# Expert 1's low parts on VectorE, counting products later, and each place finished within the next place's gate and up products

## The chip, the cores and the metric

The kernel runs on one core of a Trainium2 chip. The metric is the device time in microseconds (us) of one execution. The engines are named as in the profile: PE (TensorE), DVE (VectorE), ACT (ScalarE), POOL (GpSimd) and SP (SyncE). POOL, SP and ACT also issue DMAs.

## The reference

One decoder layer over 2,048 tokens and 16 meta tokens, all in float32, width 1,024. After a mixer come a residual sum, a normalization, routing, 16 small experts, and a last normalization:

```
g_sel = argmax(g_logits)                          # one of 4 groups
top_p, top_i = top_k(softmax(e_logits of that group), 2)   # two of its 4 experts
weights = p_g * top_p / sum(top_p)
for e in range(16):
    h = silu(xt @ w_gate[e]) * (xt @ w_up[e])     # 1024 -> 256
    y = y + combine[:, e:e+1] * (h @ w_down[e])   # 256 -> 1024
out = rmsnorm(h + y, final_norm_w)[:, 16:]
```

So each token goes through two experts, and its output can be normalized only when both have been added.

## The kernel before, in words

PE multiplies at a reduced precision, so every float32 operand is split into a high part (rounded, mostly on ACT, L107 and L111) and a low part (the remainder, L108 and L112, on DVE), and each product is three matmuls: high by high, low by high, high by low.

The first two thirds of the time are the mixer and the routing, over 16 token tiles of 128. `route_rest` writes for each tile the tokens' records to a table in DRAM (POOL, L690), sorted by expert and slot: for the tile's chosen experts `A` it needs the number of tokens that each expert has had before (products with `before_b` and `ones_b`), and for the last tile the total counts too (`counts`), from which `rank_experts` ranks the experts by size.

The experts then run one after the other in "places" 0 to 15. Places 0 and 1 are experts 0 and 1, the others are ordered by count. Places below 10 have three row tiles (128, 128 and 64 tokens), the others two. For a place

- `load_places` (SP) loads its part of the table to SBUF, `fix_words` (DVE, L1115 to L1121) turns the words into row numbers: word 1 for a token's first expert, word 2 for its second,
- `gather` (POOL, L924) fetches the tokens' rows, xg<-hn_dram,
- `transposes` (PE L946) turns them, with the split on ACT (L107) and DVE (L108),
- `gate_up` computes the hidden values in two halves f = 0, 1 (PE L975 to L977; then ACT L981, DVE L982, and the split of the hidden value: high on ACT L957, low on DVE L959 and L961),
- `down` does the down products for all row tiles, first with half 0 and then with half 1 (PE L1036 to L1041), with the result weighted and copied out by ACT (L1052) or DVE (L1054) into a row tile `xr`; when a row tile is complete POOL scatters the rows of first experts into a DRAM accumulator, oe<-xr, and gathers-and-adds that accumulator to the rows, xr<-oe,
- `square` (ACT L1072) sums the squares of the result, and `finish` (DVE: L1089, a reciprocal square root by L59 to L67, then L1078) scales it; POOL stores it, out_dram<-xr.

Rows that are not wanted have row numbers out of range, so every place issues all of these. There are six `xr` row tiles. PSUM banks are few and named: mm (two), sp, o, ds, tp, zg, m2 (shown as m). The transposes of the next place use tp and zg, which the down products use too.

The call `between(i)` inside the products of a place does the next place's transposes, one split of raw weights (`split_chunk`: ACT L111, DVE L112) and its loads. Places 0 and 1 start early: their first 13 token tiles' rows are gathered before the routing ends (`gate_rows(0, 0)`, `gate_rows(0, 2)`, then place 1's), and their second row tile (`gate_rows(0, 1)`) once all tables are there. Four of expert 1's weight chunks are split with the low part on POOL. A scheduler sets the final order of instructions on each engine; `must_follow` adds a wait.

Of the kernel before, what the change touches and what calls it, by code (L numbers as in the profile page):

```python
# [12 lines left out]
OP = mybir.AluOpType  # L13
# [4 lines left out]
NT = 16  # L18
# [3 lines left out]
NE = 16  # L22
# [48 lines left out]
def body(ctx, tc, I, O):  # L71
    nc = tc.nc
    V = nc.vector
# [14 lines left out]
    def must_follow(ins, earlier):  # L88
        for o_ in earlier:
            tc.add_manual_dep(ins.ins, o_.ins.name,  # L90
                              mybir.DependencyInfo(mybir.DependencyClass.Sync, mybir.DependencyReason.DATA),
                              reason="rows written through indices")
# [63 lines left out]
    iota16 = iota("iota16", 16, 1)  # L156
    FIXED = 2
# [462 lines left out]
    def route_rest(t):  # L620
# [9 lines left out]
        if t == EARLY + 1:  # L630
            nc.tensor.matmul(pp[:, 1], ones_b, acc[i % 2], start=True, stop=True)
            early = pp[:, 1]
            V.tensor_copy(counts, early)
            for row, at in ((late1, 128.0), (late2, float(SMALL)), (late3, float(CAP))):
                V.tensor_scalar(row[:, FIXED:], early[:, FIXED:], -1.0, at, op0=OP.mult, op1=OP.add)
            V.tensor_scalar(late2[:, :FIXED], early[:, :FIXED], -1.0, float(CAP), op0=OP.mult, op1=OP.add)
            V.tensor_scalar(late2[:, :FIXED], late2[:, :FIXED], 128.0, None, op0=OP.min)
            V.tensor_copy(late3[:, :FIXED], late2[:, :FIXED])
            V.scalar_tensor_tensor(late0[:, FIXED:], early[:, FIXED:], 48.0, iota16[:, FIXED:], op0=OP.mult, op1=OP.add)
        elif t == NT:  # L640
            nc.tensor.matmul(pp[:, 1], ones_b, acc[i % 2], start=True, stop=False)
            nc.tensor.matmul(pp[:, 1], ones_b, A, start=False, stop=True)
            V.tensor_tensor(counts, pp[:, 1], counts, op=OP.add)
        pp = pp[:, 0]
        picked[0] = nc.tensor.matmul(pp, before_b, A, start=True, stop=(t == EARLY + 1))
        if t != EARLY + 1:
            nc.tensor.matmul(pp, ones_b, acc[i % 2], start=False, stop=True)
        ngm, eg, sg, nm1, p2, den, w = T("ngm", 1), T("eg", 4), T("sg", 1), T("nm1", 1), T("p2", 1), T("den", 1), T("w", 2)
        V.tensor_scalar(ngm, gm, -1.0, None, op0=OP.mult)
        nc.scalar.activation(eg, lg[:, 0:4], AF.Exp, bias=ngm, accum_out=sg)  # L650
# [114 lines left out]
    def split_chunk(eng=None):  # L765
        r = chunks[done[0]]
        kind, e, i = stream[done[0]]
        done[0] += 1
        if kind == "d":
            hi, lo = DW[i]  # L770
        else:
            hi, lo = WP[i] if e % 2 == 0 else (WB[i][h][:, :1024] for h in range(2))
        return split(hi, lo, r, eng)
# [130 lines left out]
    with ExitStack() as c2:  # L904
# [82 lines left out]
        def gate_rows(e, j, tag, between=None):  # L987

            n, p = rows[j], bank(tag)
            for k in range(KB):  # L990
                if between:
                    between(k)
                wh, wl = gate_slot(e, k)
                xh, xl = (x[:, cols[j]:cols[j] + n] for x in XE[e % 2][k])
                nc.tensor.matmul(p[:n], xh, wh, start=(k == 0), stop=False)
                nc.tensor.matmul(p[:n], xl, wh, start=False, stop=False)
                gate_ops[k] = nc.tensor.matmul(p[:n], xh, wl, start=False, stop=(k == KB - 1))
            return j, p
# [70 lines left out]
        def square(e, j):  # L1069
            n = rows[j]  # L1070
            sq = mk.tile([128, D], BF, name="sq")
            s_ = nc.scalar.activation(sq[:n], RT[e][j][:n], AF.Square, accum_out=SS[e % 2][:n, part[j]:part[j] + 1])  # L1072
            if e + 2 < NE:
                must_follow(s_, hidden_done)
# [60 lines left out]
            for k in range(KB):  # L1135
                transposes(0, k, (0, 2), added[0])
        early = [gate_rows(0, 0, "mm"), gate_rows(0, 2, "mm", lambda k: k < 6 or transposes(1, k - 6, (0, 2)))]
        must_follow(picked[0], [gate_ops[2]])
        for k in range(4):
            split_chunk(nc.gpsimd)  # L1140
            load_chunks(min(8 + k, 10))
        for k in range(2, KB):
            transposes(1, k, (0, 2))
        load_places(0, FIXED, slice(0, FIXED))
        fix_words(0, FIXED, iota16)
        for e in range(FIXED, NE):
            load_places(e, e + 1, expert(e))
        first_rows = [ind(XG[e][1], hn_dram, col(e, 1, 0), False) for e in range(2)]
# [16 lines left out]
                    transposes(0, i, (1,))  # L1165

        early_1 = [gate_rows(1, 0, "sp"), gate_rows(1, 2, "o", early_rest)]
        down(0, (0, 2))
        for e in range(NE):
            def between(i):  # L1170
                if e + 1 < NE and i % 2 == 0:
                    for k in range(i, i + 2):
                        transposes(e + 1, k, None if e else (1,))
                if e == 0:
                    if i in (2, 6):
                        fix_words(*((2, 9) if i == 2 else (9, 16)), place)
                    if i == 0:
                        for op in load_chunks(10 + WRB, mk):
                            must_follow(op, first_rows)
                else:  # L1180
                    if done[0] < len(stream) and (i < 2 if e == NE - 1 else i in (0, 1, 2, 3, 4, 6)):
                        gate = stream[done[0]][0] == "g"
                        for op in split_chunk():
                            if gate:
                                must_follow(op, hidden_done)
                        load_chunks(done[0] + WRB, mk)
                if e >= NE - 2 and i == 1:
                    RT[e] = [row_tile(True) for j in JS[e]]
                    for j in JS[e]:
                        add_oe(e, ind(RT[e][j][:rows[j]], oe, col(e, j, 0), False), True)  # L1190
            if e == NE - 1:
                first = gate_rows(e, 0, "mm", between)
                second = gate_rows(e, 1, "mm", lambda k: k != 3 or hidden_rows(*first))
                with tc.high_priority():
                    hidden_rows(*second)
                down(e, (0,))
                down(e, (1,))
                break
            if e > 1:
                gate_up(e, between)  # L1200
            else:
                late_rows = gate_rows(e, 1, "mm", between)
                for j, p in (early_1 if e else []) + [late_rows]:
                    hidden_rows(j, p)
            if e + 3 < NE:
                gather(e + 3)
            if e > 1:
                for j in JS[e - 1]:
                    square(e - 1, j)
            if e == NE - 2:  # L1210
                finish(e - 1)
            down(e, None if e else (1,))
            if 1 < e < NE - 2:
                finish(e - 1)
            if e == 8:
                count_left(mk)

# [132 lines left out]
```

## Time and profile before

| | |
|---|---|
| timed, median of 3 | 1127.59 us (1126.79 to 1127.94) |
| profiled execution | 1121.29 us, span 1119.5 us |
| PE busy | 1055.8 us (94%) |
| DVE busy | 779.8 us (70%) |
| ACT busy | 565.7 us (51%) |
| POOL busy | 313.8 us (28%) |

The span is that of the profiled execution, from its first to its last instruction; what lies around it makes up the rest of that execution's time. Issuing a DMA on POOL shows as a busy time of its own (L690, L924), its landing comes later and is given with the DMA issues.

### The profile page before, as it was taken

How to read it: one execution, taken by the hardware profiler on the slowest of the kernel's cores; microseconds unless marked ns; L12 is line 12 of the kernel's file. 1: busy time of each engine (PE TensorE's matmuls, PEld its weight loads, DVE VectorE, ACT ScalarE, POOL GpSimd, SP SyncE). 2: the span in 40 equal slices, each digit the busy share in tenths (PEclk: the TensorE clock that was granted, in tenths of full speed). 3: DMA queues.
4: the chain of work that ended last, by engine and by line, in shares of the span. 5: the costliest groups of instructions: out<-in, count | busy, mean ns of one | idle time of the engine just before them, and what ended most of it. 6: DMA issues, size and time to landing. Idle time of an engine off the chain costs nothing. (4 is left out here: it accounts for less than half of the span.)

```text
span 1119.5 us, 19115 instructions
## 1 busy us (share of the span) xinstructions
PE 1055.8 (94%) x6614; PEld 946.5 (85%) x6614; DVE 779.8 (70%) x2649; ACT 565.7 (51%) x1192; POOL 313.8 (28%) x276
## 2 busy tenths in 40 slices
PE   7999999999999999999999998879999999989982
PEld 5888888888888889999999998558998899988861
DVE  6476666545555776878777788747787788867873
ACT  7545444334433643333333334337767777667741
POOL 2000000000000000121111105524677777776551
PEclk9999999999999999999999999989999999989996
DMA  8412332111121352533434344488888997889852
GB/s 279 166 66 76 107 101 90 62 57 48 67 85 57 115 196 67 170 142 120 145 124 151 114 153 160 132 235 237 221 248 230 242 264 214 231 256 311 255 152 74
DMA packets 64471, 174.09 MB, mean 156 GB/s; under 512 B 21012, under 2 KB 21317, under 8 KB 64368
## 3 DMA queue, kind: packets, MB, share of 16 engines
q1 hardware_dynamic: 36272, 105.72, 27.7%
q0 software_dynamic: 25504, 58.53, 20.0%
q10 hardware_dynamic: 2592, 8.55, 2.1%
q8 instruction: 54, 0.88, 0.3%
q14 instruction: 49, 0.40, 0.1%
HBM read 143.74 MB, written 57.74 MB: 180 GB/s over the span
## 5 line engine op out<-in xcount | busy, mean ns | idle before, releaser
L441 POOL DMA_DIRECT2D y_dram<-y x16 | 8.6, 541 | 391.2 <-DVE y L439 391.2
L924 POOL DMA_INDIRECT oe<-xr,tab x40 | 69.3, 1732 | 69.0 <-ACT xr L1052 57.3
L321 PE MATMUL mm<-wb,XL 128*128 128x512 f32 (+1 forms) x240 | 83.6, 348 | 0.0
L322 PE MATMUL mm<-wb,XH 128*128 128x512 f32 (+1 forms) x240 | 83.0, 346 | 0.0
L690 POOL DMA_INDIRECT table<-rec,ix x32 | 33.3, 1042 | 176.8 <-DVE tmp L703 85.4
L320 PE MATMUL mm<-wb,XH 128*128 128x512 f32 (+1 forms) x240 | 82.2, 342 | 0.0
L924 POOL DMA_INDIRECT xr<-oe,tab x39 | 75.4, 1932 | 17.8 <-issue 9.8
L523 PE MATMUL mm<-XL,ws 128*128 128x256 f32 (+1 forms) x256 | 73.0, 285 | 0.2 <-DVE XL L112 0.2
L522 PE MATMUL mm<-XH,ws 128*128 128x256 f32 (+1 forms) x256 | 73.0, 286 | 0.0
L524 PE MATMUL mm<-XH,ws 128*128 128x256 f32 (+1 forms) x256 | 72.2, 282 | 0.0
L111 ACT ACTIVATE XH<-xt 128x1024 fp32r<-128x1024 f32 x32 | 33.8, 1058 | 56.4 <-PE mm L524 36.0
L924 POOL DMA_INDIRECT out_dram<-xr,tab x39 | 55.6, 1426 | 20.8 <-DVE sr_y L60 7.4
L975 PE MATMUL mm<-xh,ws 128*128 128x320 f32 (+1 forms) x168 | 51.3, 306 | 0.0
L976 PE MATMUL mm<-xl,ws 128*128 128x320 f32 (+1 forms) x168 | 51.2, 305 | 0.0
L977 PE MATMUL mm<-xh,ws 128*128 128x320 f32 (+1 forms) x168 | 51.0, 304 | 0.0
L320 PE MATMUL mm<-ws,XH 128*128 128x512 f32 x112 | 47.4, 423 | 2.0 <-ACT XH L111 2.0
L321 PEld LDWEIGHTS mm<-wb,XL 128*128 128x128 f32 x240 | 45.4, 189 | 4.4
L1078 DVE SCALAR_TENSOR_TENSOR xr<-xr,sr_y,fw 128x1024 f32<-128x1024 f32 (+1 forms) x39 | 48.7, 1278 | 0.5
L320 PEld LDWEIGHTS mm<-wb,XH 128*128 128x128 f32 x240 | 45.1, 188 | 4.6
L322 PEld LDWEIGHTS mm<-wb,XH 128*128 128x128 f32 x240 | 45.1, 188 | 4.5
L523 PEld LDWEIGHTS mm<-XL,ws 128*128 128x128 f32 x256 | 48.1, 188 | 0.7 <-DVE XL L112 0.4
L524 PEld LDWEIGHTS mm<-XH,ws 128*128 128x128 f32 x256 | 48.4, 189 | 0.3 <-issue 0.2
(654 smaller groups left out, 3840.8 us busy)
## 6 DMA issues: line engine op xcount, KB each, us to landing
raw<-in_wgu_e_dram SPq DMA_DIRECT2D x42, 512.0 KB, 5.2
xt<-in_xT_dram SPq DMA_DIRECT2D x32, 512.0 KB, 3.5
xn<-in_xn_dram SPq DMA_DIRECT2D x32, 512.0 KB, 3.5
wr<-in_wgu_e_dram SPq DMA_DIRECT2D x22, 512.0 KB, 5.9
raw<-in_wd_e_dram SPq DMA_DIRECT2D x20, 512.0 KB, 5.6
hn_dram<-xn ACTq DMA_DIRECT2D x16, 512.0 KB, 3.3
oe<-xn POOLq DMA_DIRECT2D x16, 512.0 KB, 3.7
wr<-in_wd_e_dram SPq DMA_DIRECT2D x12, 512.0 KB, 5.8
```

The lines of the kernel that those rows point to most:

```text
L111: return (nc.scalar.activation(hi, src, AF.Copy), (eng or V).tensor_tensor(lo, src, hi.bitcast(F32), op=OP.subtract))
L320: nc.tensor.matmul(q, xh[:, k, :], wh[:, c0:c1_], start=(k == 0), stop=False)
L321: nc.tensor.matmul(q, xl[:, k, :], wh[:, c0:c1_], start=False, stop=False)
L322: nc.tensor.matmul(q, xh[:, k, :], wl[:, c0:c1_], start=False, stop=(k == KB - 1))
L522: nc.tensor.matmul(ps[:, b], WS[k][0][:, c], XH[:, k, o:], start=(k == 0), stop=False)
L523: nc.tensor.matmul(ps[:, b], WS[k][0][:, c], XL[:, k, o:], start=False, stop=False)
L524: nc.tensor.matmul(ps[:, b], WS[k][1][:, c], XH[:, k, o:], start=False, stop=(k == KB - 1))
L924: return nc.gpsimd.indirect_dma_start(out=out_, out_offset=off if scatter else None, in_=in_, in_offset=None if scatter else off, bounds_c ...
L975: nc.tensor.matmul(p[:, c0:c1_], wh, xh, start=(k == 0), stop=False)
L976: nc.tensor.matmul(p[:, c0:c1_], wh, xl, start=False, stop=False)
L977: nc.tensor.matmul(p[:, c0:c1_], wl, xh, start=False, stop=(k == KB - 1))
L1078: V.scalar_tensor_tensor(x[:n], x[:n], r[:n], fw[:n], op0=OP.mult, op1=OP.mult)
```

## The change

In `route_rest`, the two counting products of the last tile come after the products that give the slots, and the marked product of the last tile (`picked`) follows step 6 of the steps 0 to 7 of `gate_rows(0, 2)` (`gate_ops[6]`) where it followed step 2. The four splits of expert 1's weights have their low parts on DVE, and wait for the end of the routing. `fix_words` for places 0 and 1 comes later in the code, that for places 2 to 15 within place 1's products, not place 0's. `square` and `finish` of place e-1 are called within `gate_up` of place e, before the sixth and the seventh of its eight steps, for e from 2 to 14; before, `square` was called after `gate_up` and `finish` after `down` (for place 14 before it).

```diff
@@ -637,14 +637,14 @@
             V.tensor_scalar(late2[:, :FIXED], late2[:, :FIXED], 128.0, None, op0=OP.min)
             V.tensor_copy(late3[:, :FIXED], late2[:, :FIXED])
             V.scalar_tensor_tensor(late0[:, FIXED:], early[:, FIXED:], 48.0, iota16[:, FIXED:], op0=OP.mult, op1=OP.add)
-        elif t == NT:
-            nc.tensor.matmul(pp[:, 1], ones_b, acc[i % 2], start=True, stop=False)
-            nc.tensor.matmul(pp[:, 1], ones_b, A, start=False, stop=True)
-            V.tensor_tensor(counts, pp[:, 1], counts, op=OP.add)
-        pp = pp[:, 0]
+        total, pp = pp[:, 1], pp[:, 0]
         picked[0] = nc.tensor.matmul(pp, before_b, A, start=True, stop=(t == EARLY + 1))
         if t != EARLY + 1:
             nc.tensor.matmul(pp, ones_b, acc[i % 2], start=False, stop=True)
+        if t == NT:
+            nc.tensor.matmul(total, ones_b, acc[i % 2], start=True, stop=False)
+            nc.tensor.matmul(total, ones_b, A, start=False, stop=True)
+            V.tensor_tensor(counts, total, counts, op=OP.add)
         ngm, eg, sg, nm1, p2, den, w = T("ngm", 1), T("eg", 4), T("sg", 1), T("nm1", 1), T("p2", 1), T("den", 1), T("w", 2)
         V.tensor_scalar(ngm, gm, -1.0, None, op0=OP.mult)
         nc.scalar.activation(eg, lg[:, 0:4], AF.Exp, bias=ngm, accum_out=sg)
@@ -1135,14 +1135,13 @@
             for k in range(KB):
                 transposes(0, k, (0, 2), added[0])
         early = [gate_rows(0, 0, "mm"), gate_rows(0, 2, "mm", lambda k: k < 6 or transposes(1, k - 6, (0, 2)))]
-        must_follow(picked[0], [gate_ops[2]])
+        must_follow(picked[0], [gate_ops[6]])
         for k in range(4):
-            split_chunk(nc.gpsimd)
+            must_follow(split_chunk()[1], [routed])
             load_chunks(min(8 + k, 10))
         for k in range(2, KB):
             transposes(1, k, (0, 2))
         load_places(0, FIXED, slice(0, FIXED))
-        fix_words(0, FIXED, iota16)
         for e in range(FIXED, NE):
             load_places(e, e + 1, expert(e))
         first_rows = [ind(XG[e][1], hn_dram, col(e, 1, 0), False) for e in range(2)]
@@ -1165,15 +1164,16 @@
                     transposes(0, i, (1,))
 
         early_1 = [gate_rows(1, 0, "sp"), gate_rows(1, 2, "o", early_rest)]
+        fix_words(0, FIXED, iota16)
         down(0, (0, 2))
         for e in range(NE):
             def between(i):
                 if e + 1 < NE and i % 2 == 0:
                     for k in range(i, i + 2):
                         transposes(e + 1, k, None if e else (1,))
+                if e == 1 and i in (2, 6):
+                    fix_words(*((2, 9) if i == 2 else (9, 16)), place)
                 if e == 0:
-                    if i in (2, 6):
-                        fix_words(*((2, 9) if i == 2 else (9, 16)), place)
                     if i == 0:
                         for op in load_chunks(10 + WRB, mk):
                             must_follow(op, first_rows)
@@ -1184,6 +1184,11 @@
                             if gate:
                                 must_follow(op, hidden_done)
                         load_chunks(done[0] + WRB, mk)
+                if 1 < e < NE - 1 and i == 5:
+                    for j in JS[e - 1]:
+                        square(e - 1, j)
+                if 1 < e < NE - 1 and i == 6:
+                    finish(e - 1)
                 if e >= NE - 2 and i == 1:
                     RT[e] = [row_tile(True) for j in JS[e]]
                     for j in JS[e]:
@@ -1204,14 +1209,7 @@
                     hidden_rows(j, p)
             if e + 3 < NE:
                 gather(e + 3)
-            if e > 1:
-                for j in JS[e - 1]:
-                    square(e - 1, j)
-            if e == NE - 2:
-                finish(e - 1)
             down(e, None if e else (1,))
-            if 1 < e < NE - 2:
-                finish(e - 1)
             if e == 8:
                 count_left(mk)
 
```

What the change does to the order at three places follows; DMA rows name the destination and the source.

On DVE, between the routing and place 0's second row tile: L108 on `xl` of 128 columns are the eight low parts of that tile's transposes, and L1115 of 336 columns starts `fix_words` for places 2 to 8. Before:

```order
L1004 TENSOR_TENSOR h<-mm,h 64x256
L112 TENSOR_TENSOR HB<-tp,HB 128x2x64
L1115 TENSOR_TENSOR sq<-tab,iota_114 128x336
L108 SCALAR_TENSOR_TENSOR xl_8621<-zg,vecs,xh_8620 128x128
L108 SCALAR_TENSOR_TENSOR xl_8621<-tp,vecs,xh_8620 128x128
L1116 TENSOR_TENSOR sq<-sq,place 128x336
```

With the change:

```order
L1004 TENSOR_TENSOR h<-mm,h 64x256
L108 SCALAR_TENSOR_TENSOR xl_8621<-zg,vecs,xh_8620 128x128
L112 TENSOR_TENSOR HB<-tp,HB 128x2x64
L108 SCALAR_TENSOR_TENSOR xl_8621<-zg,vecs,xh_8620 128x128
L108 SCALAR_TENSOR_TENSOR xl_8621<-tp,vecs,xh_8620 128x128
L1115 TENSOR_TENSOR sq<-tab,iota_114 128x336
L108 SCALAR_TENSOR_TENSOR xl_8621<-zg,vecs,xh_8620 128x128
L1116 TENSOR_TENSOR sq<-sq,place 128x336
```

Three of the eight low parts have moved ahead of L1115; before, all eight stood behind it.

On POOL, one place of the steady part: the scatters and gathers of a place e, and the three stores (x3) of place e-1. Before:

```order
L924 DMA oe<-xr,tab 2048x1024
L924 DMA xr<-oe,tab 128x1024
L924 DMA oe<-xr,tab 2048x1024
L924 DMA xr<-oe,tab 128x1024
L924 DMA oe<-xr,tab 2048x1024
L924 DMA xr<-oe,tab 64x1024
L924 DMA out_dram<-xr,tab 2048x1024 x3
```

With the change:

```order
L924 DMA out_dram<-xr,tab 2048x1024 x3
L924 DMA oe<-xr,tab 2048x1024
L924 DMA xr<-oe,tab 128x1024
L924 DMA oe<-xr,tab 2048x1024
L924 DMA xr<-oe,tab 128x1024
L924 DMA oe<-xr,tab 2048x1024
L924 DMA xr<-oe,tab 64x1024
```

The three stores have moved from behind the six scatters and gathers to ahead of them. So it is for places 2 to 7; from place 8 on, the stores stand behind the first scatter, or the first scatter and gather.

On ACT and DVE, the same part: the second half of a place's hidden value (ACT L981, L957; DVE L982, L959, L961), the squares (L1072) and the finish (L1089 to L1078) of the place before. ACT before, and with the change:

```order
L981 ACTIVATE h<-mm 128x320
L107 ACTIVATE xh_8620<-tp,vecs 128x320
L107 ACTIVATE xh_8620<-zg,vecs 128x320
L957 ACTIVATE HB<-h 128x320
L1072 ACTIVATE sq,SS_8877<-xr 128x1024
```

```order
L981 ACTIVATE h<-mm 128x320
L1072 ACTIVATE sq,SS_8869<-xr 128x1024
L107 ACTIVATE xh_8620<-tp,vecs 128x320
L1072 ACTIVATE sq,SS_8869<-xr 64x1024
L107 ACTIVATE xh_8620<-zg,vecs 128x320
L957 ACTIVATE HB<-h 128x320
```

DVE with the change:

```order
L1089 SCALAR_TENSOR_TENSOR ms<-SS_8869,tab 128x3
L59 TENSOR_SCALAR sr_y<-ms 128x3
L60 TENSOR_SCALAR sr_y<-sr_y 128x3
L108 SCALAR_TENSOR_TENSOR xl_8621<-zg,vecs,xh_8620 128x320
L982 TENSOR_TENSOR h<-m_10370,h 128x320
L65 TENSOR_TENSOR sr_t<-sr_y 128x3
L66 TENSOR_TENSOR sr_t<-sr_t,ms 128x3
L67 SCALAR_TENSOR_TENSOR sr_y<-sr_t,sr_y 128x3
L65 TENSOR_TENSOR sr_t<-sr_y 128x3
L959 TENSOR_TENSOR HB<-h,HB 128x256
L961 TENSOR_TENSOR HB<-h,HB 128x64
L66 TENSOR_TENSOR sr_t<-sr_t,ms 128x3
```

On ACT the third square, which needs the third gather of the place before, now stands ahead of the hidden value's high part (L957). On DVE the hidden value's L982, L959 and L961, which stood ahead of L1089 and next to each other, now stand behind it.

## Rows read from the trace of the kernel before

**Rows 1.** By stretch: busy us of PE, PEld, DVE, ACT, POOL; clock, DMA, GB/s.

```profile
900.00:980.00 80.00, 79.63 (x516) 73.45 (x516) 67.03 (x143) 58.09 (x100) 57.98 (x37) 1.00 0.83 231
```

**Rows 2.** Timeline of PE: start, us, operation, idle before, its releaser.

```profile
708.67 0.17 PE L642 MATMUL m<-A,ones_b 128*128 128x16 bf16 x1 [2.70 <-DVE A L615]
...
735.34 0.47 PE L946 MATMUL zg<-ident,xg 128*128 128x128 f32 x1 [7.04 <-DVE xl L108]
...
744.83 0.48 PE L995 MATMUL mm<-ws,xh 128*128 128x512 f32 x1
```

**Rows 3.** Timeline of POOL, end of routing.

```profile
695.47 2.43 POOL L112 TENSOR_TENSOR wb<-raw,wb 128x1024 fp32r<-128x1024 f32 x1 [6.59 <-PE ds L572]
```

**Rows 4.** Timeline of DVE, routing to the second half of expert 0.

```profile
696.61 1.32 DVE L663 TENSOR_TENSOR v<-v,late 128x16 f32<-128x16 f32 x1
...
697.93 2.29 DVE L665 TENSOR_TENSOR t<-t,step 128x16 f32<-128x16 f32 x1
...
700.23 2.35 DVE L667 TENSOR_TENSOR t<-lev,late_step 128x16 f32<-128x16 f32 x1
...
708.97 2.28 DVE L685 TENSOR_SCALAR rec<-w,rs_r 128x2 f32<-128x2 f32 x1
...
711.60 0.16 DVE L665 TENSOR_TENSOR t<-t,step 128x16 f32<-128x16 f32 x1
...
715.04 1.22 DVE L112 TENSOR_TENSOR wb<-raw,wb 128x1024 fp32r<-128x1024 f32 x1
...
734.51 0.51 DVE L1115 TENSOR_TENSOR sq<-tab,iota 128x336 f32<-128x336 f32 x1 [7.33 <-DMA tab<-table]
```

**Rows 5.** Timeline of PE, places 7, 9 and 13.

```profile
913.14 0.39 PE L1036 MATMUL sp<-wb,HB 128*128 128x512 f32 x1
...
916.84 0.40 PE L1036 MATMUL sp<-wb,HB 128*128 128x512 f32 x1
...
961.82 0.39 PE L1036 MATMUL sp<-wb,HB 128*128 128x512 f32 x1
...
1048.64 0.39 PE L1036 MATMUL sp<-wb,HB 128*128 128x512 f32 x1
```

**Rows 6.** Timeline of POOL, places 1, 6 and 8.

```profile
786.45 1.73 POOL L924 DMA_INDIRECT xr<-oe,tab  x1 [0.30 <-issue]
...
895.81 1.59 POOL L924 DMA_INDIRECT oe<-xr,tab  x1 [2.91 <-ACT xr L1052]
...
906.75 1.74 POOL L924 DMA_INDIRECT xr<-oe,tab  x1 [0.30 <-issue]
...
908.79 1.04 POOL L924 DMA_INDIRECT out_dram<-xr,tab  x1 [0.30 <-issue]
...
911.99 1.76 POOL L924 DMA_INDIRECT out_dram<-xr,tab  x1 [0.30 <-DVE xl L108]
...
945.32 1.61 POOL L924 DMA_INDIRECT oe<-xr,tab  x1 [4.17 <-ACT xr L1052]
...
954.99 2.99 POOL L924 DMA_INDIRECT xr<-oe,tab  x1 [0.30 <-issue]
```

**Rows 7.** Issue to landing, us: 740 to 980, at 786.45, at 954.99.

```profile
xr<-oe,tab POOLq DMA_INDIRECT x26, 6.1
...
xr<-oe,tab POOLq DMA_INDIRECT x1, 7.9
...
xr<-oe,tab POOLq DMA_INDIRECT x1, 5.1
```

**Rows 8.** Timeline of ACT, third square of place 6.

```profile
918.58 1.04 ACT L1072 ACTIVATE sq<-xr 64x1024 bf16<-64x1024 f32 x1
```

**Rows 9.** Timeline of DVE, hidden low, then finish of place 6.

```profile
914.71 0.22 DVE L961 TENSOR_TENSOR HB<-h,HB 128x64 fp32r<-128x64 f32 x1
...
919.75 0.16 DVE L1089 SCALAR_TENSOR_TENSOR ms<-SS,tab 128x3 f32<-128x3 f32 x1 [1.42 <-ACT sq L1072]
...
922.16 1.28 DVE L1078 SCALAR_TENSOR_TENSOR xr<-xr,sr_y,fw 128x1024 f32<-128x1024 f32 x1
```

## The prediction, made before the changed kernel was run

> **What bounds the kernel now.** I read the busy time by stretch first, then the timelines of PE, DVE, POOL and ACT, and last the landing times of the DMAs. In the steady part of the experts PE is the bound: 79.63 us of 80 are busy, at full clock, while DVE, ACT and POOL have slack [rows 1]. There, time is lost or won only by making PE wait, so each edit has to be read by what PE waits for after it. The other place is the end of the routing, where PE already waits: for a counting product, and then 7.04 us for a low part of a transpose [rows 2].
>
> At the end of the routing the slow engine is DVE. From 695.47 POOL makes expert 1's low parts, one in 2.43 us [rows 3], and in that time DVE operations on 16 columns take 1.32, 2.29 and 2.35 us, later one more 2.28 us; the same line L665 takes 0.16 us when POOL is not at it [rows 4]. The late routing makes the tables late, and DVE's L1115 stands waiting for them until 734.51 [rows 4], with the low parts that PE wants behind it.
>
> In the steady part the reader should see a chain that is almost, but not quite, a loop. For place 6 the first scatter-add is issued at 895.81 and the third gather-add at 906.75 [rows 6]; such a gather lands 6.1 us after its issue in the median [rows 7], so at 912.9. Place 7's gate and up products end where its down products begin, at 913.14 [rows 5]. The results of one place land just when the next place's products end. Today nothing on PE's path waits for that landing: the squares come after the products, the finish (L1089) starts at 919.75 [rows 9], and the three stores to the output are issued behind all six scatters and gathers, from 908.79 [rows 6].
>
> **The change part by part.** *Lows to DVE.* POOL's four go, and with them the four slow rows: 1.32 + 2.29 + 2.35 + 2.28 - 4 x 0.16 = 7.6 us of DVE [rows 4]. Four lows of 1.22 us [rows 4] come in, three of them in a row at the routing's end: 3 x 1.22 = 3.7 us. The tables come 7.6 - 3.7 = 3.9 us earlier, and so does L1115 of places 2 to 8. Three of the eight low parts of expert 0's second tile now stand ahead of it (the order above), so of the 10.32 us from L1115 at 734.51 to the products of that tile at 744.83 [rows 4, 2] three eighths, 3.9 us, are done before the wait ends. Gain 7.8 us; bounds: 3.9 us if the reordering brings nothing, and 3.9 + 7.04 = 10.9 us if PE's wait at 735.34 goes altogether [rows 2].
>
> *Lows against POOL's DMAs.* What the trace shows is one direction, POOL's low slowing DVE from 0.16 to 2.29 us [rows 3, 4]. The Trainium skill (page "SBUF — State Buffer", section "Who interferes with whom") states that a DVE instruction with two SBUF inputs and a GpSimd instruction that reads SBUF exclude each other for the whole of the first. The trace agrees as far as L665 goes. By this rule the new lows would in turn hold POOL's table writes, by up to the 3.7 us of the three, and the gain would be 4.1 us, not 7.8 us. I do not take that, since no row shows a DMA issue held so.
>
> *Counting products.* The two now follow the 42 gate products of expert 0; PE's wait of 2.70 us for the second one [rows 2] goes. I count nothing more for it: PE comes earlier to the same L1115, which sets when expert 0's second tile can start. The work that hides it is DVE's table chain; without that cover it would be worth that 2.70 us.
>
> *Squares and finish inside the next place.* Here the order matters more than the text. Call L the landing of a place's third gather. Third square on ACT, 1.17 us from its start to L1089 on DVE [rows 8, 9]; L1089 to the first L1078 is 2.41 us for twelve small operations, 0.2 us each [rows 9]. Now the next place's hidden low (L982 to L961) stands in the middle of those, and ahead of it on ACT its HB (L957) stands behind the third square. So the low comes after L by: 1.17, three small operations 0.6, one low part of a transpose taken at 0.5 (an estimate, between the 0.16 and 1.22 us of rows 4), and 1.6 us for the low itself (today it ends at 914.93, 1.8 us after the first down product's start at 913.14, and the last gate product still runs some 0.2 us into that [rows 5, 9]); together L + 3.9. The second half of the down products needs it, 916.84 - 913.14 = 3.70 us after their first [rows 5]. Before, that was always met; now PE waits as soon as L is later than the first down product's start less 0.2 us.
>
> That alone would cost little. But the finish sends out its stores sooner, and on POOL they now stand ahead of the next place's first scatter. After L + 3.9 come five small operations, 1.0, and a first L1078 of 1.28 [rows 9]: first store at L + 6.2. Three stores keep POOL from 906.75 + 1.74 to 911.99 + 1.76, which is 5.3 us [rows 6], and with 0.3 us of issue the next place's first scatter comes at L + 11.8. From there to its third gather's landing is 906.75 - 895.81 + 6.1 = 17.0 us [rows 6, 7]. So a loop closes: one landing to the next takes 11.8 + 17.0 = **28.8 us**, and PE's down products wait in it at every turn.
>
> Its sum: place 1's third gather lands at 786.45 + 7.9 = 794.35 [rows 6, 7]. Seven turns later, for place 8, it is 794.35 + 7 x 28.8 = 995.95, and place 9's second half of the down products begins 3.9 us behind, at 999.85. Before, it began at 961.82 + 3.70 = 965.52 [rows 5]. The cost up to place 9 is **34.3 us**. Places 10 to 13 have two row tiles. Their loop is shorter by a pair (12.68 / 3 = 4.2 us from 895.81 to 908.49) and a store (5.3 / 3 = 1.8 us), so 22.8 us; before, a place took (1048.64 - 961.82) / 4 = 21.7 us, stalls included [rows 5, 6]. Four times 1.1 is **4.4 us**. The remaining order on POOL (stores behind the first scatter from place 8 on) I take as equal, since POOL issues the same either way. The last two places keep their form.
>
> Bounds of the turn. Low: place 8's took 954.99 + 5.1 - 945.32 = 14.8 us from scatter to landing, and three stores at 1.04 + 0.30 us are 4.0 us, so 10.5 + 14.8 = 25.3 us. High: with the landing of 7.9 us, 30.6 us [rows 6, 7]. I stay at 28.8: place 6's issues and the median landing are nearest to what most places show.
>
> **Sum.** -7.8 + 34.3 + 4.4 = +30.9 us. The profiled execution took 1121.29 us (a span of 1119.5 us), and would come to 1152.2 us. It lies 6.3 us below the median of the timed runs, 1127.59 us, so for these I say **1158 us**.
>
> **The rivals.** *The loop does not bind.* The cost is -7.8 + (7 T - 167.2) + 4 (T - 27.7) for a turn of T, which is zero at T = 26.0 us: a turn shorter than that makes the change faster. At the low bound, 25.3 us, it gives -7.6 us, about 1120 us; with the early gain between 3.9 and 10.9 us 1117 to 1124 us. For it: POOL idles 2.91 us and 4.17 us ahead of the first scatters [rows 6], so stores that are ready in time would fill a hole. Against it: they are ready only at L + 6.2. Chance 0.22.
>
> *A longer turn.* More of the DMAs' time (their share is 0.83 already [rows 1]) or ACT's weight parts ahead of the evacuation lengthen the turn to the high bound of 30.6 us: 11 x 1.8 = 20 us more, 1178 us. For it: place 1's landing took 7.9 us [rows 7]. Against it: PE's waits thin the traffic. Chance 0.08.
>
> *The new lows hold POOL's table writes.* POOL's low slowed DVE fourteenfold [rows 3, 4]; if DVE's three lows hold POOL's writes as long as they run, the early gain falls by 3.7 us and the time is 1162 us. For it: L665 at 2.29 us. Against it: that a DMA's issue is held as an arithmetic operation is, no row shows. Chance 0.12. It is the rule of the Trainium skill's page "SBUF — State Buffer" named above.
>
> **Chances and range.** The forecast (a turn that binds, between 27 and 30 us, 1137 to 1171 us) has 0.48, the held writes, in the same range, 0.12; turns between 26 and 27 us, with 1127 to 1137 us, 0.10; the faster case 0.22, the longer turn 0.08. About 0.2% is what a measurement of this kernel can tell from no change. Of the two cases around zero 0.05 fall within it, so: faster 0.22, same 0.05, slower 0.73. The range reaches from 1117 us, the low end of the faster case, to 1174 us, inside the longer turn; forecast alone: 1137 to 1171 us.
>
> **What the next profile would show.** Right: no POOL L112, L665 and L667 at 0.16 us near 697, the second tile of expert 0 some 8 us earlier; L959 or L961 as the releaser of a PE wait in L1037 in every place from 2 to 9; the third square (L1072) idle for the gather; the first oe<-xr of a place 11 to 12 us after the landing, behind three stores; places 3 to 8 about 4 us longer. Wrong: PE at 79 of 80 us as before in the steady part, and landings well ahead of the products' end. The prediction falls if POOL's stores are issued before the evacuation is ready, so that no scatter waits, or if the landing shortens by 3 us as the stores move.

## The result and the profile after

The changed kernel takes 1163.38 us in the median (1158.92 to 1164.39, 4 runs) beside 1127.19 us for the kernel before on the same chip (4 runs): a ratio of 1.0314, 95% interval 1.0286 to 1.0342, 3.1% slower. The profiled execution took 1163.58 us with a span of 1161.8 us, 42.3 us more than the span before; the timed medians lie 36.2 us apart, since the execution profiled before took 1121.29 us, less than any of those four runs. The forecast was 1158 us, a cost of 31 us.

The first view is the busy time by stretch (columns as in [rows 1]); its first line answers to that row. The third line is the kernel before in the later stretch.

```profile
900.00:980.00 80.00, 72.13 (x423) 62.45 (x422) 59.87 (x132) 51.79 (x87) 50.82 (x31) 0.98 0.74 214
980.00:1060.00 80.00, 66.07 (x423) 57.90 (x422) 52.51 (x102) 48.36 (x84) 43.83 (x31) 0.91 0.78 228
...
980.00:1060.00 80.00, 72.50 (x491) 66.01 (x491) 59.93 (x122) 55.90 (x100) 49.77 (x32) 0.96 0.89 282
```

PE is idle for 8 us of 80 in the steady part, where it was idle for 0.4 us before. In the next stretch it is idle for 14 us, at a granted clock of 0.91; before, for 7.5 us, at 0.96. No other engine is busier than before: 50.82 us on POOL here, 57.98 us before. So PE waits, and its list of waits from 740 to 1120 (what it waited for, us in total, times, the longest) says for what:

```profile
PE sp L1036 <- ACT HB L957: 12.5, 5, 4.3
PE zg L1040 <- DVE xl L108: 10.3, 7, 2.5
PE tp L946 <- ACT xr L1052: 8.5, 8, 1.6
PE tp L1036 <- DVE xl L108: 8.0, 6, 2.4
PE sp L1037 <- DVE HB L959: 1.5, 4, 0.5
```

The largest sums are the hidden high (L957) and the low parts of transposes (L108): ACT and DVE instructions that stand behind the third square and the finish. All five waits for the hidden high lie in the places with two row tiles, from 1017.57 on; up to place 9 it is mostly the low parts, and banks (tp) that ACT has not yet copied out. The wait for L959, which I had named as the mark, is 1.5 us only; in the steady part the order is met one link earlier, on banks tp and zg in the first half of the down products.

One turn of the ring, from timelines of POOL, ACT, DVE, POOL, ACT and PE, place 4 to place 5:

```profile
857.34 1.59 POOL L924 DMA_INDIRECT oe<-xr,tab  x1 [0.30 <-issue]
...
868.04 1.45 POOL L924 DMA_INDIRECT xr<-oe,tab  x1 [0.30 <-issue]
...
873.47 1.06 ACT L1072 ACTIVATE sq<-xr 64x1024 bf16<-64x1024 f32 x1 [0.53 <-DMA xr<-oe,tab]
...
876.11 0.47 ACT L957 ACTIVATE HB<-h 128x320 fp32r<-128x320 f32 x1 [1.07 <-DVE h L982]
...
874.66 0.16 DVE L1089 SCALAR_TENSOR_TENSOR ms<-SS,tab 128x3 f32<-128x3 f32 x1 [1.13 <-ACT sq L1072]
...
876.99 0.22 DVE L961 TENSOR_TENSOR HB<-h,HB 128x64 fp32r<-128x64 f32 x1
...
878.09 1.29 DVE L1078 SCALAR_TENSOR_TENSOR xr<-xr,sr_y,fw 128x1024 f32<-128x1024 f32 x1
...
879.66 1.81 POOL L924 DMA_INDIRECT out_dram<-xr,tab  x1 [5.82 <-DVE xr L1078]
...
885.21 0.92 POOL L924 DMA_INDIRECT out_dram<-xr,tab  x1 [0.31 <-issue]
...
886.44 1.58 POOL L924 DMA_INDIRECT oe<-xr,tab  x1 [0.30 <-issue]
...
880.15 0.67 ACT L1052 ACTIVATE xr<-sp,tab 128x512 f32<-128x512 f32 x1
...
873.59 0.50 PE L1036 MATMUL tp<-wb,HB 128*128 128x512 f32 x1 [1.03 <-DVE xl L108]
...
875.74 0.51 PE L1040 MATMUL zg<-wb,HB 128*128 128x512 f32 x1 [1.19 <-DVE xl L108]
...
880.72 0.30 PE L975 MATMUL mm<-xh,ws 128*128 128x320 f32 x1
882.60 0.33 PE L946 MATMUL tp<-ident,xs 128*128 128x128 f32 x1 [1.58 <-ACT xr L1052]
```

Place 4's first scatter goes out at 857.34 and its third gather at 868.04. ACT's third square starts with its landing at 873.47, the releaser being that DMA: L. L1089 follows at L + 1.2, the hidden low ends at L + 3.7, the first store is issued at L + 6.2. The three stores hold POOL to 886.13, and the next first scatter is at 886.44, L + 13.0. ACT's evacuation was ready sooner: its first copy starts at 880.15. From scatter to landing it is 16.1 us, so the turn is 29.1 us. Over the five turns from place 2 (first scatter at 800.05) to place 7 (943.58) the mean is 28.7 us. PE meets it in three small waits, 1.03, 1.19 and 1.58 us. In this place they are 3.8 us together.

The last of the three is in part due to something else, which the section on the change does not show: the scheduler moved PE's transposes of the next place too. The first of them (L946 on tp) now stands behind one gate product of a place (880.72), where it stood behind seven before. There it needed no wait, as in place 7:

```profile
896.83 0.27 PE L946 MATMUL tp<-ident,xs 128*128 128x128 f32 x1
```

The early edits, in DVE, POOL and PE rows ([rows 2] and [rows 4] answer to them):

```profile
700.69 0.17 DVE L665 TENSOR_TENSOR t<-t,step 128x16 f32<-128x16 f32 x1
...
714.05 1.22 DVE L112 TENSOR_TENSOR wb<-raw,wb 128x1024 fp32r<-128x1024 f32 x1
...
714.93 1.20 POOL L690 DMA_INDIRECT table<-rec,ix  x1 [0.30 <-issue]
...
715.32 0.50 PE L997 MATMUL sp<-wb,wb 128*128 128x512 f32 x1 [2.25 <-DVE wb L112]
...
739.83 0.48 PE L995 MATMUL mm<-ws,xh 128*128 128x512 f32 x1
```

L665 is at 0.17 us (2.29 before). DVE's new lows take 1.22 us, and a table write issued beside them takes 1.20 us. PE waits 2.25 us for the first of them. This execution came to its first gate products at 699.69, the one before at 695.77, so the products of expert 0's second tile at 739.83 are 40.1 us behind, not 49.1 us: a gain of 8.9 us. In the run of the early edits alone (below) they are 37.3 us behind (732.63 - 695.32), a gain of 11.8 us; so this gain differs from one execution to another.

And the two-row places, POOL, ACT, POOL, and PE's first down products of place 9 (two halves) and of place 13 ([rows 5]):

```profile
1048.89 1.62 POOL L924 DMA_INDIRECT oe<-xr,tab  x1 [10.43 <-ACT xr L1052]
...
1059.51 2.02 POOL L924 DMA_INDIRECT xr<-oe,tab  x1 [0.30 <-issue]
...
1068.25 1.06 ACT L1072 ACTIVATE sq<-xr 128x1024 bf16<-128x1024 f32 x1 [0.36 <-DMA xr<-oe,tab]
...
1074.99 1.83 POOL L924 DMA_INDIRECT oe<-xr,tab  x1 [10.78 <-ACT xr L1052]
...
983.77 0.39 PE L1036 MATMUL sp<-wb,HB 128*128 128x512 f32 x1
...
990.29 0.44 PE L1036 MATMUL sp<-wb,HB 128*128 128x512 f32 x1
...
1088.64 0.39 PE L1036 MATMUL sp<-wb,HB 128*128 128x512 f32 x1
```

The turn from 1048.89 to 1074.99 is 26.1 us: the last gather is issued 10.6 us behind the first scatter, lands 8.7 us later, and the next scatter comes 6.7 us after that. Here the stores stand behind the first scatter, and it is not for them that the next one waits: POOL waits 10.43 and 10.78 us for ACT to copy out PE's results, so the ring passes through PE.

By stretch, profiled span against profiled span: +3.9 us ahead of the experts (a difference between executions: the runs below with the same early edits reach expert 0's first gate products at 695.3 to 697.2 us, this one at 699.69), -8.9 us to expert 0's second tile, +29.8 us from there to place 9's second half (990.29 - 739.83 against 965.52 - 744.83), +15.2 us to place 13 (98.35 against 83.12 us), +2.3 us to the end.

The 15.2 us are not all waiting. The same 538 products of PE lie in that stretch before (first line) and after:

```profile
965.52:1048.64 83.12, 76.55 (x538) 71.03 (x536) 64.81 (x127) 58.90 (x104) 56.33 (x35) 0.96 0.89 273
...
990.29:1088.64 98.35, 82.46 (x538) 73.22 (x538) 65.00 (x126) 58.42 (x99) 50.79 (x34) 0.90 0.80 235
```

PE is busy 5.9 us longer with them, at a mean granted clock of 0.90 against 0.96, and idle 9.3 us longer. From 1068.9 to 1075.6, in the turn shown, the granted clock was 0.50, the lower of its two levels (1.2 GHz).

### The profile page after: what moved, and what is told of

The parts are those of the page before. It is cut to its first block, busy times and chain, and to the rows that moved or that the text cites. A ratio compares the mean times of both kernels' runs of the same rounds, so it can differ in the third digit from the quotient of the medians.

```text
span 1161.8 us, 19160 instructions
## 1 busy us (share of the span) xinstructions
PE 1072.6 (92%) x6614; PEld 950.9 (82%) x6614; DVE 778.4 (67%) x2653; ACT 565.6 (49%) x1192; POOL 300.8 (26%) x272
## 5 line engine op out<-in xcount | busy, mean ns | idle before, releaser
L924 POOL DMA_INDIRECT out_dram<-xr,tab x39 | 61.0, 1563 | 57.9 <-DVE xr L1078 40.2
L924 POOL DMA_INDIRECT xr<-oe,tab x39 | 65.6, 1682 | 19.0 <-issue 11.0
L1072 ACT ACTIVATE sq<-xr 128x1024 bf16<-128x1024 f32 (+1 forms) x35 | 36.9, 1056 | 58.4 <-DMA xr<-oe,tab 53.9
L112 DVE TENSOR_TENSOR wb<-raw,wb 128x1024 fp32r<-128x1024 f32 x39 | 47.4, 1218 | 16.3 <-ACT wb L111 16.3
L108 DVE SCALAR_TENSOR_TENSOR xl<-tp,vecs,xh 128x320 fp32r<-128x320 f32 (+3 forms) x45 | 22.0, 489 | 44.4 <-ACT xh L107 36.9
```

The lines of the kernel that those rows point to most:

```text
L112: (eng or V).tensor_tensor(lo, src, hi.bitcast(F32), op=OP.subtract))
L924: return nc.gpsimd.indirect_dma_start(out=out_, out_offset=off if scatter else None, in_=in_, in_offset=None if scatter else off, bounds_c ...
```

## Experiments

The ring (scatter, gather, landing, square, finish, stores, next scatter) is my theory; its rivals are that the early edits cost later, that ACT's or DVE's order alone makes PE wait, or that the loss is one of the places with two row tiles. The diffs are against the changed kernel where not said otherwise. Ratios are to the kernel before on the same chip, with 95% intervals; it took 1122 to 1123 us beside these runs, so runs are compared by their ratios.

**Either part alone.** The first run puts the squares and the finish back:

```diff
-                if 1 < e < NE - 1 and i == 5:
-                    for j in JS[e - 1]:
-                        square(e - 1, j)
-                if 1 < e < NE - 1 and i == 6:
-                    finish(e - 1)
...
+            if e > 1:
+                for j in JS[e - 1]:
+                    square(e - 1, j)
+            if e == NE - 2:
+                finish(e - 1)
             down(e, None if e else (1,))
+            if 1 < e < NE - 2:
+                finish(e - 1)
```

> The lows on DVE, the later counting products and the later slot words stay; squares and finish are back where they were before. By the loop theory (each place's third gather, squares, finish and stores stand in a ring with the next place's first scatter) the whole loss goes and the early gain alone is left: about 5 us, the shift seen at expert 0's second tile (739.83 against 744.83 us), so 1122 us. The rival, that the early edits cost something later too (lows on DVE in the way, slot words late), has the time at or above the 1127 us of before.

Measured 1112.26 us, ratio 0.9913 (0.9888 to 0.9939): 9.8 us faster than before, twice the gain expected. Its windows, 820 to 900 us, show PE full again:

```profile
820.00:900.00 80.00, 79.09 (x499) 72.95 (x498) 64.97 (x121) 57.96 (x96) 63.24 (x40) 1.00 0.88 237
```

The second run is the kernel before with only these lines moved.

> Only squares and finish inside the next place's products; the start of the experts as before. Loop theory: the loop sets the period whatever the start, so the time is that of the full change plus the 5 us of early gain, about 1168 us. Rival: the full change's loss comes from both parts together (the lows on DVE pushing the finish back), then this is well below 1163 us.

Measured 1170.77 us, 1.0431 (1.0399 to 1.0463). So the whole loss, and more, is in the squares and the finish; the early edits gain 0.9% without them and 1.2% beside them.

**Stores off the ring.** The scaled rows stay where the change put them, but POOL's stores are queued behind the next place's last gather:

```diff
             for j in JS[e]:
-                scale_out(e, j, r[:, part[j]:part[j] + 1])
+                n, x = rows[j], RT[e][j]
+                V.scalar_tensor_tensor(x[:n], x[:n], r[:n, part[j]:part[j] + 1], fw[:n], op0=OP.mult, op1=OP.mult)
+                later.append((e, j, x))
...
             down(e, None if e else (1,))
+            while later:
+                store(*later.pop(0))
+                queued_after(out_ops[-1], oe_ops[-1][1])
```

> All of the change, but the stores of a finished place are queued on POOL behind the next place's scatters and gathers, as before the change. Squares and finish stand on ACT and DVE as in the full change. Loop theory: without the stores the first scatter comes about 8 us after the landing, not 13, and the turn is 8 + 16.5 = 24.5 us, just inside PE's 24.75 us: steady places near 25 us, and 1125 to 1138 us in all. Rival, that the third square's wait on ACT and the finish on DVE by themselves make the loss: places stay at 28 us and the time above 1150 us.

Measured 1132.29 us, 1.0097 (1.0066 to 1.0128): two thirds of the loss are gone (from 36 us to 11 us above before), or a good half if the early edits alone are taken as the base (from 45 us to 20 us above them). POOL, ACT and POOL, one turn:

```profile
864.92 2.71 POOL L924 DMA_INDIRECT oe<-xr,tab  x1 [3.73 <-ACT xr L1052]
...
876.34 1.44 POOL L924 DMA_INDIRECT xr<-oe,tab  x1 [0.31 <-issue]
...
882.59 1.05 ACT L1072 ACTIVATE sq<-xr 64x1024 bf16<-64x1024 f32 x1
...
889.29 0.68 ACT L1052 ACTIVATE xr<-sp,tab 128x512 f32<-128x512 f32 x1
...
890.82 2.68 POOL L924 DMA_INDIRECT oe<-xr,tab  x1 [4.06 <-ACT xr L1052]
```

Third square at 882.59, first copy at 889.29, next scatter at 890.82: 8.2 us from square to scatter, not 13.0 us, and the turn is 25.9 us, a little over PE's 24.75 us of before. Against the early edits alone 1.8% (20 us) are left, more than the theory had. PE's waits of this run, from 740 to 1120, say where:

```profile
PE tp L946 <- ACT xr L1052: 9.7, 9, 1.4
PE sp L1036 <- ACT HB L957: 9.2, 5, 4.4
```

The first sum is mostly the wait of the next place's first transposes, about 1.2 us at the start of each of the places 3 to 10. They come after one gate product in the steady part and not after seven, and ACT copies their bank out later: in the turn shown from 891.00, 0.9 us behind the place's first gate product (890.06), before from 896.01, 0.2 us behind it (895.80). So this part comes of the scheduler's order on PE and ACT. The second sum, for the hidden high behind the squares, lies from place 9's down products on (five waits from 987.98). No run takes the two apart.

**Finish behind the hidden low.** Here DVE does the finish later, and the stores come to stand between the first pair and the second:

```diff
-                if 1 < e < NE - 1 and i == 6:
-                    finish(e - 1)
...
+            if 1 < e < NE - 1:
+                finish(e - 1)
             down(e, None if e else (1,))
...
+            queued_after(s_, hidden_done[0])
             r = seed_rstd(nc, mk, ms, 3)
```

Here `s_` is L1089.

> All of the change, but on DVE the finish is queued behind the next place's hidden low; the squares stay ahead on ACT, and the stores now stand on POOL behind the first scatter and gather, ahead of the other two pairs. Loop theory: the stores are still in the ring, since the second and third gather wait behind them, and the turn stays at 28 to 29 us: 1155 to 1168 us. Rival, that the finish's operations ahead of the hidden low are the cost: the low comes 1 to 2 us earlier in each of 12 places and the time falls to 1140 us or below.

Measured 1169.89 us, 1.0411 (1.0376 to 1.0445). POOL, ACT, POOL of one turn:

```profile
848.88 1.91 POOL L924 DMA_INDIRECT oe<-xr,tab  x1 [8.20 <-ACT xr L1052]
...
853.87 1.03 POOL L924 DMA_INDIRECT out_dram<-xr,tab  x1 [0.31 <-issue]
...
864.51 1.69 POOL L924 DMA_INDIRECT xr<-oe,tab  x1 [0.30 <-issue]
...
872.04 1.06 ACT L1072 ACTIVATE sq<-xr 64x1024 bf16<-64x1024 f32 x1 [5.48 <-DMA xr<-oe,tab]
...
880.14 2.05 POOL L924 DMA_INDIRECT oe<-xr,tab  x1 [10.03 <-ACT xr L1052]
```

The stores are inside the ring, issued from 853.87 on between the first scatter and the third gather, and the turn is 31.3 us; turn and time lie above what was expected. With the finish out of the hidden low's way, but the stores still in the ring, nothing is won. So DVE's order alone does not make the loss. What it would be worth with the stores off the ring, no run shows.

**The early edits apart.** The kernel before with only the lows moved (`split_chunk(nc.gpsimd)` to `must_follow(split_chunk()[1], [routed])`):

> Only expert 1's lows on DVE after the routing; counting products, slot words, squares and finish as before. My account of the early gain: DVE's four slow rows (7.6 us) go, three lows (3.7 us) come, so 3.9 us from the tables alone, and 4 to 8 us with the counting products' waits, which also come from the slow DVE rows: 0.4 to 0.7% faster. Rival (the rule of exclusion taken both ways): the lows hold POOL's table writes by up to 3.7 us, and nothing is gained.

Measured 1111.59 us, 0.9903 (0.9877 to 0.993). And the kernel before with only the counting products and slot words later:

> Only the counting products and the slot words later; lows stay on POOL. My account: DVE stays slow, so the tables come no sooner; PE's two counting waits go but are given back in the wait for the tables: 0 to 3 us faster. Rival: the early gain of the two together (10 us) comes from PE's order, and most of it shows here.

Measured 1120.67 us, 0.9983 (0.997 to 0.9995). The lows are the gain, 11 us, above the 4 to 8 us expected; the other edit gives 2 us alone and nothing measurable on top.

**By place.** The condition `1 < e < NE - 1` becomes `1 < e < LARGE`, with the old lines for the rest:

> The early edits, and squares and finish inside the next place's products only for the places with three row tiles (finishing places 1 to 8); the others as in the run of the early edits alone. Loop theory: turns of 28 to 29 us against PE's 24.75 us, eight of them, so 30 to 36 us slower than the early edits alone, about 1.9% slower than before. Rival (the loss sits in the two-row places, where the measured period was most above the forecast): under 20 us.

Measured 1139.88 us, 1.014 (1.0105 to 1.0176), which is 2.3% or 26 us above the early edits alone. That lies between the theory (30 to 36 us) and its rival (under 20 us). In the profile place 10's products begin 33 us later (989.58 against 956.25), so the turns cost what the theory says; from there to the end of the span 3 us are won back. With `LARGE <= e < NE - 1` instead:

> The early edits, and squares and finish inside only from place 10 on (finishing places 9 to 13). Loop theory, with the turn of 26 us that the full change showed there against 21.7 us before: 8 to 17 us slower than the early edits alone, so from the same as before to 0.6% slower. By the 22.8 us of my forecast it would be 4 us. Rival: sooner stores free row tiles, whose wait (3.8 us of PE) goes, and this is faster than the early edits alone.

Measured 1120.08 us, 0.9974 (0.996 to 0.9989), 0.6% or 7 us above the early edits alone, just under what was expected. The rival falls: no gain over the early edits. The two parts together are 2.9%, the full change 4.0%. That the two-row places have no slack left when both hold would explain the rest; it is argued, not shown.

**One operation more on the ring.** The third square is done twice (`for j in JS[e - 1] + JS[e - 1][-1:]`), in the full change:

> The full change with the last row tile's square done twice in each place, 1.04 us more on ACT behind the landing and ahead of the hidden high and the finish; the result is the same. Loop theory: this lengthens each turn by 1.0 to 1.2 us, and there are 13 turns: 11 to 15 us slower than the full change, about 4.2% slower than before. Rival (the loss is set by the landings alone, with ACT idle in its wait and able to hide an operation): under 4 us more than the full change.

Measured 1176.59 us, 1.0482 (1.0456 to 1.0509): 1.7% or 19 us above the full change, for 13 operations of 1.04 us, and more than the 11 to 15 us expected. So nothing hides the operation. But the excess is not its price alone, since two more things differ in this trace. The scheduler put the three stores behind the first scatter (scatter at 851.57, stores from 853.57 on), where the full change has them ahead of it. And from place 2's first down product to place 9's second half PE is busy 191.70 us with the same 1,076 products, at a mean granted clock of 0.92, where the full change has 184.26 us at 0.98. The same on top of the early edits alone, where squares follow the products:

> The same doubled square with squares and finish where they were before (early edits kept). Loop theory: no ring closes here and PE waits for nothing behind the square, so within 3 us of the early edits alone, 0.6 to 0.9% faster than before. Rival (any microsecond of ACT between products and evacuation costs PE): 10 us slower than the early edits alone.

Measured 1103.7 us, 0.9823 (0.9803 to 0.9843). Not only no cost, but 10 us faster than the early edits alone; neither theory had that. PE's waits from 780 to 1100, of the early edits alone and of this one:

```profile
PE tp L946 <- ACT xr L1052: 5.4, 2, 3.8
```

```profile
PE zg L1007 <- DVE h L1004: 3.6, 1, 3.6
PE zg L946 <- DVE xl L108: 3.2, 1, 3.2
```

The 5.4 us of waiting for banks that ACT had to copy out are gone; a wait of 3.2 us for a low part has come. The two profiled executions lie only 2.2 us apart (spans of 1108.0 and 1105.8 us), so these traces show a small part of the 10 us. The scheduler had drawn up another order around the doubled square: the next place's first transposes come 14 to 24 gate products into a place, not 7, and from place 9 on other things moved too. Whether the first of these is the cause, the last run asked.

```diff
-                if e + 1 < NE and i % 2 == 0:
-                    for k in range(i, i + 2):
+                at = {2: 0, 3: 2, 4: 4, 6: 6}.get(i) if e > 1 else i if i % 2 == 0 else None
+                if e + 1 < NE and at is not None:
+                    for k in range(at, at + 2):
```

> The early edits, with squares and finish where they were before and no doubled square; the first two transposes of the next place come after 24 gate products of a place instead of 7 and 20. It tests why the doubled square outside made the kernel faster: there the scheduler had moved these transposes from behind 7 products to behind 14 to 24, and PE's waits for the banks tp and zg at the start of a place (0.3 us in six places, 3.75 us at place 10, 1.7 us at place 12) were gone. If that order is the cause: 5 to 12 us faster than the early edits alone, 1.3 to 1.9% faster than before. Rival (the spacing of ACT's evacuation by the second square is the cause): no faster than the early edits alone, 0.7 to 0.9% faster than before.

Measured 1115.86 us, 0.9933 (0.9915 to 0.9951), no faster than the early edits alone. ACT's wait and PE's, of this run:

```profile
ACT xr L1052 <- DMA out_dram<-xr,tab: 7.2, 4, 5.1
...
PE tp L946 <- ACT xr L1052: 4.4, 1, 4.4
```

The row tile of place 10 is still waited for, by ACT for the store's landing and by PE behind it. So first transposes that come later are not enough. The built order is not that of the doubled square either: in most places with three row tiles the second transposes come after 50 gate products here, after 21 to 31 there. Why the doubled square outside is faster stays open.

**Sooner stores for two places.** On the early edits, `if e == NE - 2` ahead of `down` becomes `if e in (10, 11, NE - 2)`:

> The early edits, and for places 10 and 11 alone the finish of the place before comes ahead of the down products, with squares still behind the gate and up products, so that PE waits for nothing in them. Meant to free place 9's and 10's row tiles sooner, whose stores' landing made PE wait 3.8 us at place 11. If that wait is real time: 2 to 4 us faster than the early edits alone (1.1 to 1.3% faster than before). Rival: the stores ahead of the scatter delay this place's own rows and the wait comes back elsewhere: no gain or a few us lost.

Measured 1113.64 us, 0.9925 (0.9901 to 0.9948): no gain. PE's longest wait for a bank that ACT still has to copy out stayed at 3.8 us.

The best of all runs is the early edits with the doubled square outside, 1.8% faster than before; among those with no superfluous work the lows alone and the early edits together, 1.0% and 0.9%, which the runs don't tell apart.

## Why the prediction was right

**The ring.** Forecast 28.8 us a turn, measured 28.7 us in the mean of five; its two halves were each off by about a microsecond and cancelled: landing to scatter 13.0 us (forecast 11.8 us, since three stores took 6.5 us and not 5.3 us), scatter to landing 16.1 us (forecast 17.0 us). L + 3.9 for the hidden low was 3.7 us, L + 6.2 for the first store 6.2 us. That the stores' place on POOL carries a good half of the loss is shown by moving them alone, and that all of it lies in the squares and the finish by either part alone.

**Up to place 9.** Forecast 34.3 us, measured 29.8 us: the same turns, but place 1's third gather, issued at 780.72, landed 5.3 us later (its square starts at 786.05) and not 7.9 us, and place 9's second half began 2.4 us behind place 8's third square (987.90), not 3.9 us. Where PE waits was named wrongly in part: I had the hidden low in the second half of the down products; up to place 9 it was the low parts of the next place's transposes, for banks of the first half, and the first of those transposes themselves, which the scheduler had moved ahead; in the two-row places it was the hidden high. The low parts and the hidden high stand behind the same square.

**Places 10 to 13.** The term that was mis-sized: "4.4 us" for four places, measured 15.2 us. "Their loop is shorter by a pair and a store, so 22.8 us" took over the median landing of the steady part, 6.1 us, and took the stores behind the first scatter as equal to stores ahead of it. The last gather landed 8.7 us behind its issue there, and in the run with the stores behind it all, first scatters of two-row places still came 22.5 to 26.2 us apart. Nor does the first scatter wait for stores there: it waits for PE's results to be copied out, so PE's own pace is in the ring, and 5.9 us of the 15.2 us are time in which PE was busy, at the lower granted clock. The prediction has no term for that. In the two-row places alone the edit costs 7 us; why it costs more in the full change is not shown.

**The early edits.** Forecast 7.8 us, measured 8.9 and 11.8 us in two traces and 10 us in time. The step "I count nothing more for it" for the counting waits held for the edit as such (2 us alone), but those waits vanish with the slow DVE rows: with the lows alone the second one is down from 2.70 to 0.3 us.

The rival by exclusion came, but at a small price. That "no row shows a DMA issue held so" overlooks a row of the kernel before, beside the DVE low at 715.04 [rows 4]:

```profile
715.36 1.76 POOL L690 DMA_INDIRECT table<-rec,ix  x1 [0.30 <-DVE t L724]
```

This table write was issued with 0.9 us of the low (715.04 + 1.22) still to come and took 1.76 us (1.75 us in the run of the squares and the finish alone); the seven writes ahead of it took 0.99 to 1.04 us. In the changed kernel one write was issued while a low ran, with 0.3 us of it left, and took 1.20 us: 0.2 us lost, where three lows in full would have cost 3.7 us. The rule of the Trainium skill (page "SBUF — State Buffer", section "Who interferes with whom"), that DVE's two-input instruction and a GpSimd instruction that reads SBUF exclude each other, agrees with the way L665 fell from 2.29 to 0.17 us when POOL's lows went. For a DMA's issue the prediction took that rule further than the page does: the same section of the Trainium skill's page infers that a tensor_tensor does not hold it. The two writes here took longer beside one, and so the measurement decides.

The range (1117 to 1174 us) and the sign held, and the mechanism of the steady part is the one forecast. That the total came so close is partly luck: 4 us too much up to place 9 and 11 us too little behind it are errors of opposite sign, and the halves of the turn cancelled as well.

## What to carry to other kernels

Work moved into the cover of a busy engine is free only if its inputs arrive ahead of what stands behind it in the same queue: here three in-order queues (ACT, DVE, POOL) took one late landing into the next place, and handed it on. Add up the whole ring, landing to landing, and compare it with the period; here a ring 4 us longer than the period (28.7 us against 24.75 us) cost 4 us at every turn. And read the built order of every engine: stores that used to fill a hole behind the scatters made a good half of the loss, and PE's transposes had moved too, which I had not read.

## What the runs showed that was not expected

A superfluous operation made the kernel faster: 1.04 us more of ACT in each place, outside the ring, took 10 us off (0.9823 against 0.9913). The scheduler's order changed with it, but why it is faster stays open. The same operation on the ring cost 19 us for 13 turns, with another order of the stores and a lower granted clock beside it. Moving elementwise work off POOL was worth 11 us although it added 4.9 us to DVE: four POOL operations had held four small DVE ones for 7.6 us, and PE had waited twice for 2.7 us behind them. How the 11 us divide between these is not shown.
